# Retention with wide q and k and split output products; another order in two projections; conversions queued behind the MLP's residual

## The chip, the cores and the metric

The kernel runs on one NeuronCore of a Trainium2 chip. The metric is device microseconds for one execution. Times of the kernel before are the median of three runs; the rows further down come from one more execution, which was profiled.

## The reference, cut to what matters

One sequence of 256 tokens with 1024 features passes a block of four token mixers with a squared-ReLU MLP, then a retention layer with a SwiGLU FFN, then a layer of sparse attention (NSA) with a second SwiGLU FFN. All weights are f32 and are used once. What the change touches:

```python
# end of the first block
x = x + jnp.sum(gates * branch, axis=2) @ w_out[l]              # 1024 x 1024
x = x + jnp.square(jax.nn.relu(h @ w_up[l])) @ w_down[l]        # 1024 -> 4096 -> 1024
return rms_norm(x, final_norm_g)
# retention: 4 heads, q and k of 256, v and g of 512, chunk of 128
q = rotate_pairs(q, cos, sin)
k = rotate_pairs(k, cos, sin) * (dk ** -0.5)
scores = jnp.einsum('bhid,bhjd->bhij', qc, kc) * intra_decay
o = jnp.einsum('bhij,bhje->bhie', scores, vc) + ...             # the state's part
# then o is normalised a head, multiplied by silu(g), and projected back (2048 -> 1024)
# NSA: q, three gates a head, keys and values of three branches; projected back (1024 -> 1024)
h = h + rms_norm_2(mixed, mix_norm_post[layer])
```

## The kernel before, in words

**Split products.** Nearly every product with weights is made of two parts: an operand is copied by ScalarE to a rounded f32 form (`hi`), VectorE subtracts it from the source (`lo`), and PE multiplies hi by hi, hi by lo and lo by hi (`mm3`, lines 246 to 251). These matmuls take one pass. A matmul of plain f32 operands, as in retention's scores (1136, 1138) and outputs (1164, 1166), is run as two instructions.

**Weights.** `each_half` (225 to 238) loads half a chunk of weights (512 KB) into one of four `raw` buffers through SyncE's DMA queue, ScalarE makes `whi` (234) and VectorE `wlo` (237, in one or two pieces). `whi` and `wlo` have six buffers each (`wsp`); some stages add a few of their own.

**Forms of a projection.** In `ws_tile` (253) the weights stand and the activations stream: per k-step three matmuls of 256 columns. `wide_steps` (265 to 280) makes the same of hi and lo side by side: one matmul of 512 columns (274) with `whi` and one of 256 (276) with `wlo`; the two halves of the bank are then added up by a ScalarE copy (277) and a VectorE addition (278). `an_groups` and `an_steps` let the activations stand and stream weights, 512 columns wide.

**`project_back`** (357 to 383) projects back to 1024 features: two token halves t, two banks of 512 columns each, so four accumulators. The first weight halves go to all four at once. The last three chunks, six halves, are held: t=0 runs all of them for bank 0, then all of them for bank 1, then its residual and norm (`residual`, `nxt.a`) are issued; t=1 follows with both banks for each held half, and before the last half the transposes of the next stage's input for t=0 (`nxt.b(0)`, line 436) are put. `w_out` and `w_no` have eight halves in all (`nk` = 8), `w_ro` 16, the FFNs 22, the MLP 32.

**Residuals.** `add_residual` (446) makes two VectorE additions (449), one a bank. In the MLP a norm with gain follows (406, 411, 414, 416, 1070), and then the next stage's own norm (`Inputs.a`: sums, POOL's power at 416, `xn` at 193 and 194). `Inputs.b` transposes `xn` and makes hi and lo of it (209, 210). The next stage's first weights are loaded and converted meanwhile by `an_groups` (297 to 327); it has eight halves, and in retention one buffer beyond the six.

**Retention.** After v (`w_rv`), q and k of each head are made by `ws_chunk`, rotated by three VectorE products from PSUM and one POOL addition (1124 to 1131), and the scores of the head before are put behind each q (1146). Then for each head the gate is made in four halves (`gates`), the last head's scores or the transposes of the head before follow, and `outputs` multiplies the scores `at` with `v`: one product for t=0 and two for t=1.

**NSA.** It first issues the load of its gate weights `w_ng` and their split to `wg` (1287 to 1290), then `an_groups` for keys and values and the copies of their results to `cd` and `vn` (1304, 1305). `wg` is used later, with `G` in the order of steps.

**Order.** The program's order sets priorities; a scheduler fixes each engine's order when the kernel is built, by what it holds to be ready. `issue_after(i)` makes the instructions traced within it, on i's engine, follow i there; it is an edge of order and no wait. `behind` uses it already in the first block.

Of the kernel before, what the change touches and what calls it, by code (L numbers as in the profile page):

```python
# [19 lines left out]
T = 256  # L20
D = 1024
KT = 8
# [190 lines left out]
class Kernel:  # L213
# [83 lines left out]
    def an_groups(self, groups, n, inp, order=(0, 1), extra=0):  # L297
# [3 lines left out]
        with ExitStack() as es:  # L301
            pool = self.pool(es, "ax_" + groups[0][0], extra) if extra else None
            hs = []
            for i, (name, g) in enumerate(groups):
                for j in range(4):
                    if j % 2 == 0:
                        own = {s: pool for s in range(2) if len(hs) + s + extra >= 4 * len(groups)}
                        chunk = self.each_half(name, 2 * g + j // 2, 4 * n, own, 2)
                    hs.append((i, 2 * j, next(chunk)))
# [47 lines left out]
    def project_back(self, name, nk, get, last, residual, nxt):  # L357


        accs = [[self.bank() for _ in range(2)] for _ in range(2)]  # L360
        n = nk // 2
        held = []
        with ExitStack() as es:
            wx = self.pool(es, "wx_" + name, 2 * last)
            for c in range(n):
                x, k0 = get(c)
                for s, half in enumerate(self.halves(name, c, pools={i: wx for i in range(2) if c >= n - last})):
# [4 lines left out]
                    else:  # L372
                        held.append(a)
            for t in range(2):
                for banks in ((0,), (1,)) if t == 0 or not nxt else ((0, 1),):
                    for a in held[:-1]:
                        self.as_t(accs[t], *a, t, banks)
                    if t and nxt:
                        nxt.b(0)
                    self.as_t(accs[t], *held[-1], t, banks)  # L380
# [89 lines left out]

    def behind(self, engine):
# [5 lines left out]
    def run(self):  # L477
        nc = self.nc
        with ExitStack() as es:
# [9 lines left out]
            self.ps = self.pool(es, "ps", 8, bass.MemoryType.PSUM)  # L489
            nc.scalar.preload_act_table_set("natural_log_exp_and_others")  # L490
# [540 lines left out]
    def mlp(self, inp):  # L1031
# [3 lines left out]
        with ExitStack() as es:  # L1035
# [29 lines left out]
            def residual(t, acc):  # L1065
                self.add_residual(t, acc)
                r = self.sumsq_rstd([self.x[:, t, n * 512:(n + 1) * 512] for n in range(2)], D)
# [22 lines left out]
    def retention(self, inp):  # L1090
        nc, I = self.nc, self.I
        mm = nc.tensor.matmul
        with ExitStack() as es:
# [30 lines left out]
            def rotated(s, ps):  # L1124
                a = tp.tile([128, 2, T], F32, tag=f"rot{s}", name="rot")
                b = tp.tile([128, 2, T], F32, tag="rotb", name="rotb")
                nc.vector.tensor_tensor(a, ps, cs, op=OP.mult)
                for j in range(2):
                    nc.vector.tensor_tensor(b[:, j, :], ps[:, 1 - j, :], sn[:, j, :], op=OP.mult)
# [12 lines left out]
            for h in range(4):  # L1142
                rot = []
                for s in range(2):
                    rot.append(rotated(s, self.ws_chunk("w_rqk", 2 * h + s, xin)))
                    if s == 0 and qk:
# [4 lines left out]
            def gates(g):  # L1151
                sg = tp.tile([128, 2, 512], F32, tag="sg", name="sg", bufs=1)
                for _ in self.an_steps("w_rg", g, 512, xin,
                                       lambda t, ps: nc.scalar.activation(sg[:, t, :], ps, AF.Silu)):
                    pass
                return sg

            def outputs(g, sg):
                vs = slice(g * 512, (g + 1) * 512)
# [443 lines left out]
```

## Time and profile before

| what | us |
|---|---|
| median of three runs (lowest, highest) | 1204.8 (1204.67, 1211.26) |
| the profiled execution, by the device's time | 1208.24 |
| its span, first to last instruction | 1206.5 |
| mean granted TensorE clock (of full speed) | 0.993 |

The stages lie as follows in the profiled execution: the mixers to 267 us, `w_out` to 291, the MLP to 480, retention to 690 with its q and k from 526 to 576 and the gates and outputs to 640, the first FFN to 876, NSA to 1014 with `w_no` from 987, the second FFN to the end. PE is TensorE's matmul, PEld its weight loads, DVE VectorE, ACT ScalarE, POOL GpSimd. A matmul's shown duration overlaps with the next; the distance between two starts is what one costs. PEclk is the clock that PE was granted, 1.00 for 2.4 GHz.

### The profile page before, as it was taken

How to read it: one execution, taken by the hardware profiler on the slowest of the kernel's cores; microseconds unless marked ns; L12 is line 12 of the kernel's file. 1: busy time of each engine (PE TensorE's matmuls, PEld its weight loads, DVE VectorE, ACT ScalarE, POOL GpSimd, SP SyncE). 2: the span in 40 equal slices, each digit the busy share in tenths (PEclk: the TensorE clock that was granted, in tenths of full speed). 3: DMA queues.
4: the chain of work that ended last, by engine and by line, in shares of the span. 5: the costliest groups of instructions: out<-in, count | busy, mean ns of one | idle time of the engine just before them, and what ended most of it. 6: DMA issues, size and time to landing. Idle time of an engine off the chain costs nothing.

```text
span 1206.5 us, 18129 instructions
## 1 busy us (share of the span) xinstructions
PE 1184.8 (98%) x6848; PEld 1014.4 (84%) x6848; DVE 806.3 (67%) x1413; ACT 662.9 (55%) x1148; POOL 80.8 (7%) x87
## 2 busy tenths in 40 slices
PE   8999999999999998999999999999999999999997
PEld 6999889887888887899878888888889877888886
DVE  7757877667746667557456665657778967655663
ACT  5545765655644454543555554556567876645561
POOL 1000001200000000012000000000100530000000
PEclk8999999999999999999999999999999999999999
DMA  7654454536455565554546355556655226555560
GB/s 239 196 175 158 140 191 158 175 126 230 161 192 187 191 208 181 177 194 158 166 148 213 120 192 189 192 185 212 209 194 179 72 70 205 179 189 186 189 205 35
DMA packets 60775, 210.11 MB, mean 174 GB/s; under 512 B 7120, under 2 KB 9808, under 8 KB 60560
## 3 DMA queue, kind: packets, MB, share of 16 engines
q1 hardware_dynamic: 60688, 208.95, 53.0%
q8 instruction: 54, 0.88, 0.3%
q14 instruction: 33, 0.27, 0.1%
HBM read 207.84 MB, written 1.08 MB: 173 GB/s over the span
## 4 chain that ended last, share of the span: by engine, by line
PE 82%; DVE 7%; DMA 5%; ACT 3%; issue 1%; POOL 0%; SPq 0%; DVEq 0%; POOLq 0%; ACTq 0%
PE b L274 19%; PE b L249 15%; PE b L251 15%; PE b L250 15%; PE b L276 9%; DVE wlo L237 3%; ACT whi L234 1%; PE b L436 1%; DMA raw<-w_up 1%; DMA raw<-w_no 1%; DMA raw<-w_rv 1%; PE b L1536 1%; DMA raw<-w_ck 1%; DMA wng<-w_ng 1%; ACT s L1503 1%
## 5 line engine op out<-in xcount | busy, mean ns | idle before, releaser
L237 DVE TENSOR_TENSOR wlo<-raw,whi 128x1024 fp32r<-128x1024 f32 (+3 forms) x432 | 470.9, 1103 | 265.1 <-ACT whi L234 262.2
L234 ACT ACTIVATE whi<-raw 128x1024 fp32r<-128x1024 f32 (+1 forms) x384 | 401.6, 1050 | 383.6 <-issue 116.5
L274 PE MATMUL b<-x,whi 128*128 128x512 f32 x1024 | 362.7, 398 | 0.0
L276 PE MATMUL b<-x,wlo 128*128 128x256 f32 x1024 | 286.3, 280 | 0.0
L249 PE MATMUL b<-whi,x 128*128 128x512 f32 (+1 forms) x720 | 283.9, 395 | 1.8 <-ACT x L209 1.0
L250 PE MATMUL b<-wlo,x 128*128 128x512 f32 (+1 forms) x720 | 280.7, 390 | 1.0 <-DVE wlo L237 0.8
L251 PE MATMUL b<-whi,x 128*128 128x512 f32 (+1 forms) x720 | 279.8, 390 | 0.6 <-DVE x L210 0.6
L274 PEld LDWEIGHTS b<-x,whi 128*128 128x128 f32 x1024 | 192.2, 188 | 45.9 <-issue 0.3
L276 PEld LDWEIGHTS b<-x,wlo 128*128 128x128 f32 x1024 | 193.1, 189 | 0.9
L249 PEld LDWEIGHTS b<-whi,x 128*128 128x128 f32 x720 | 136.1, 189 | 34.5 <-ACT x L209 4.3
L251 PEld LDWEIGHTS b<-whi,x 128*128 128x128 f32 x720 | 136.3, 189 | 29.9 <-DVE x L210 1.3
L250 PEld LDWEIGHTS b<-wlo,x 128*128 128x128 f32 x720 | 136.4, 189 | 28.7 <-DVE wlo L237 1.9
L249 PE MATMUL b<-x,whi 128*128 128x256 f32 x480 | 137.6, 287 | 0.0
L251 PE MATMUL b<-x,wlo 128*128 128x256 f32 x480 | 135.5, 282 | 0.4 <-DVE wlo L237 0.4
L250 PE MATMUL b<-x,whi 128*128 128x256 f32 x480 | 135.4, 282 | 0.0
L249 PEld LDWEIGHTS b<-x,whi 128*128 128x128 f32 x480 | 91.5, 191 | 2.1 <-issue 1.5
L251 PEld LDWEIGHTS b<-x,wlo 128*128 128x128 f32 x480 | 91.5, 191 | 0.6 <-DVE wlo L237 0.6
L250 PEld LDWEIGHTS b<-x,whi 128*128 128x128 f32 x480 | 91.6, 191 | 0.1
L416 POOL TENSOR_TENSOR rstd<-ms,mhalf 128x1 f32<-128x1 f32 x22 | 13.8, 626 | 686.5 <-DVE ms L414 686.5
L210 DVE SCALAR_TENSOR_TENSOR x<-b,gc,x 128x128 fp32r<-128x128 f32 x112 | 36.7, 348 | 20.2 <-ACT x L209 18.3
L209 ACT ACTIVATE x<-b,gc 128x128 fp32r<-128x128 f32 x112 | 37.9, 367 | 21.7 <-PE b L436 16.5
L1503 ACT ACTIVATE s<-s,nm 128x128 f32<-128x128 f32 (+1 forms) x64 | 28.2, 444 | 2.6 <-DVE rz L1507 1.4
(277 smaller groups left out, 1014.8 us busy)
## 6 DMA issues: line engine op xcount, KB each, us to landing
raw<-w_fi SPq DMA_DIRECT2D x88, 512.0 KB, 4.5
raw<-w_fo SPq DMA_DIRECT2D x44, 512.0 KB, 4.5
raw<-w_gate SPq DMA_DIRECT2D x32, 512.0 KB, 4.2
raw<-w_up SPq DMA_DIRECT2D x32, 512.0 KB, 3.9
raw<-w_down SPq DMA_DIRECT2D x32, 512.0 KB, 3.9
raw<-w_qk SPq DMA_DIRECT2D x24, 512.0 KB, 4.1
raw<-w_rv SPq DMA_DIRECT2D x16, 512.0 KB, 4.8
raw<-w_rqk SPq DMA_DIRECT2D x16, 512.0 KB, 4.5
```

What stands on the lines that cost most here:

```text
L209: k.nc.scalar.activation(hi, ps[:, j, :], AF.Copy, scale=g)
L210: k.nc.vector.scalar_tensor_tensor(lo, ps[:, j, :], g, hi.bitcast(F32), op0=OP.mult, op1=OP.subtract)
L234: nc.scalar.activation(hi[:, :n], r, AF.Copy)
L237: nc.vector.tensor_tensor(lo[:, c], r[:, c], hi[:, c].bitcast(F32), op=OP.subtract)
L249: mm(out, lhs[0], rhs[0], start=start, stop=False)
L250: mm(out, lhs[0], rhs[1], start=False, stop=False)
L251: mm(out, lhs[1], rhs[0], start=False, stop=stop)
L274: mm(ps.rearrange("p a t -> p (a t)"), half[0][:, s], x[2][:, k].rearrange("p a t -> p (a t)"), start=k == 0, stop=False)
L276: mm(ps[:, 0], half[1][:, s], x[0][:, k, :], start=False, stop=k == KT - 1)
L416: nc.gpsimd.tensor_tensor(r, ms, self.mhalf[:, :1], op=OP.pow)
L436: self.nc.tensor.transpose(ps[:, j, :], src[:, j * 128:(j + 1) * 128], self.ident)
L1503: nc.scalar.activation(s[:, a, i, :], s[:, a, i, :], AF.Exp, bias=nm[:, a, i:i + 1], scale=-1.0, accum_out=z[:, a, i:i + 1])
```

## The change

`project_back` runs t=0 (and t=1 of the last projection) in another order where it has eight halves: bank 0 leads bank 1 by one held weight. It resets `rows_done`; only the MLP's residual for t=0 sets it, to the last ScalarE and VectorE instructions issued so far, and `an_groups` queues the conversions of its third half and all later ones behind these two. Retention makes q and k by `ws_wide` and rotates them from SBUF; the scores of a head are put behind the next head's k (for the last head behind the second gate half). Its `gates` splits v and the scores of its head into hi and lo, in the buffers of the rotations, behind the third gate half for the first head and behind the first for the others, and `outputs` makes each product of three one-pass matmuls. NSA's split of `wg` is issued behind the copies of `cd` and `vn` and queued behind them. Loads, tiles and the rest stay as they are.

```diff
@@ an_groups
+                    queued = self.queued(self.rows_done if len(hs) > 1 else ())
                     if j % 2 == 0:
                         own = {s: pool for s in range(2) if len(hs) + s + extra >= 4 * len(groups)}
                         chunk = self.each_half(name, 2 * g + j // 2, 4 * n, own, 2)
-                    hs.append((i, 2 * j, next(chunk)))
+                    with queued:
+                        hs.append((i, 2 * j, next(chunk)))
@@ project_back
+        self.rows_done = ()
...
+            lead = min(len(held), 1 if nk == KT else len(held))
             for t in range(2):
-                for banks in ((0,), (1,)) if t == 0 or not nxt else ((0, 1),):
-                    for a in held[:-1]:
-                        self.as_t(accs[t], *a, t, banks)
-                    if t and nxt:
+                if t == 0 or not nxt:
+                    order = [(i, 0) for i in range(lead)]
+                    for i in range(len(held)):
+                        order += [(i + lead, 0)] * (i + lead < len(held)) + [(i, 1)]
+                else:
+                    order = [(i, n) for i in range(len(held)) for n in range(2)]
+                for i, n in order:
+                    if t and nxt and (i, n) == (len(held) - 1, 0):
                         nxt.b(0)
-                    self.as_t(accs[t], *held[-1], t, banks)
+                    self.as_t(accs[t], *held[i], t, (n,))
@@ new
+    def lasts(self):
+        order = list(reversed(self.nc.cur_bb.bb.instructions))
+        return [next(i for i in order if i.engine == e.engine) for e in (self.nc.scalar, self.nc.vector)]
+    def queued(self, instructions):
+        es = ExitStack()
+        for i in instructions:
+            es.enter_context(self.tc.issue_after(i))
+        return es
@@ mlp, residual
                 self.add_residual(t, acc)
+                if t == 0:
+                    self.rows_done = self.lasts()
@@ retention
-            def rotated(s, ps):
-                a = tp.tile([128, 2, T], F32, tag=f"rot{s}", name="rot")
+            def rotated(s, i):
+                a = self.ws_wide("w_rqk", i, xin, tp.tile([128, 2, T], F32, tag=f"rot{s}", name="rot"))
                 b = tp.tile([128, 2, T], F32, tag="rotb", name="rotb")
-                nc.vector.tensor_tensor(a, ps, cs, op=OP.mult)
                 for j in range(2):
-                    nc.vector.tensor_tensor(b[:, j, :], ps[:, 1 - j, :], sn[:, j, :], op=OP.mult)
+                    nc.vector.tensor_tensor(b[:, j, :], a[:, 1 - j, :], sn[:, j, :], op=OP.mult)
+                nc.vector.tensor_tensor(a, a, cs, op=OP.mult)
                 nc.gpsimd.tensor_tensor(a, a, b, op=OP.add)
...
-                    if s == 0 and qk:
+                    if s == 1 and qk:
                         scores(h - 1, *qk)
...
+                parts, steps = [], 0
                 for _ in self.an_steps("w_rg", g, 512, xin,
                                        lambda t, ps: nc.scalar.activation(sg[:, t, :], ps, AF.Silu)):
-                    pass
-                return sg
+                    steps += 1
+                    if steps == 2 and g == 0:
+                        scores(3, *qk)
+                    if steps == (3 if g == 0 else 1):
+                        src = [v[:, t, g * 512:(g + 1) * 512] for t in range(2)] + [at[:, g, :]]
+                        for tag, x in zip(("rot0", "rot1", "rotb"), src):
+                            hl = [tp.tile([128, 2, T], F32, tag=tag, name=tag).rearrange("p a t -> p (a t)").bitcast(F32R)
+                                  [:, :x.shape[1]] for _ in range(2)]
+                            self.split(*hl, x)
+                            parts.append(hl)
+                return sg, parts
...
-                    mm(p, at[:, g, t * 128:t * 128 + 128], v[:, 0, vs], start=True, stop=t == 0)
+                    self.mm3(p, [x[:, t * 128:t * 128 + 128] for x in w], v0, True, t == 0)
                     if t:
-                        mm(p, at[:, g, T:384], v[:, 1, vs], start=False, stop=True)
+                        self.mm3(p, [x[:, T:384] for x in w], v1, False, True)
@@ nsa
-            wg = tp.tile([128, KT, 96], F32R, name="wg")
-            self.split(wg[:, :, :48], wg[:, :, 48:], raw.rearrange("p (k c) -> p k c", k=KT))
...
                 nc.scalar.activation(vn[:, t, :], ps[1][t], AF.Copy)
+            wg = tp.tile([128, KT, 96], F32R, name="wg")
+            with self.queued(self.lasts()):
+                self.split(wg[:, :, :48], wg[:, :, 48:], raw.rearrange("p (k c) -> p k c", k=KT))
```

## Rows read from the trace of the kernel before

**Rows 1.** The page's first part, PE: busy us (share), count of instructions.

```profile
PE 1184.8 (98%) x6848; PEld 1014.4 (84%) x6848; DVE 806.3 (67%) x1413; ACT 662.9 (55%) x1148; POOL 80.8 (7%) x87
```

**Rows 2.** Waits of PE, whole span: who waited for whom, us, times, longest.

```profile
PE b L436 <- DVE xn L193: 7.9, 2, 4.6
PE b L249 <- ACT whi L234: 1.5, 2, 0.8
PE b L249 <- ACT x L209: 1.0, 3, 0.5
```

**Rows 3.** Timeline of PE, end of the MLP: start, us, engine, line, operation.

```profile
473.54 0.40 PE L251 MATMUL b<-whi,x 128*128 128x512 f32 x1
```

**Rows 4.** Chain of waits, 462 to 481 us: start, us, what.

```profile
468.89 1.07 ACT whi L234
...
469.98 1.29 DVE wlo L237 x2
471.27 0.61 DVE res L449
...
477.28 1.94 PE b L436 x8
479.23 0.43 PE b L249
```

**Rows 5.** Windows: stretch, length, busy us by engine, PEclk, DMA share, GB/s.

```profile
478.00:480.00 2.00, 2.00 (x9) 1.81 (x8) 0.69 (x3) 0.99 (x3) 0.00 (x0) 0.51 0.00 0
...
998.00:1002.00 4.00, 3.44 (x9) 2.66 (x10) 2.52 (x3) 1.80 (x3) 0.00 (x0) 0.60 0.78 265
```

**Rows 6.** Timeline of PE in `w_no`; in brackets the wait before.

```profile
987.36 0.50 PE L249 MATMUL b<-whi,x 128*128 128x512 f32 x1
...
995.80 0.47 PE L249 MATMUL b<-whi,x 128*128 128x512 f32 x1
997.04 0.50 PE L250 MATMUL b<-wlo,x 128*128 128x512 f32 x1 [0.76 <-DVE wlo L237]
...
998.56 1.03 PE L249 MATMUL b<-whi,x 128*128 128x512 f32 x2 [0.79 <-ACT whi L234]
...
1011.86 1.04 PE L436 MATMUL b<-cm,xn 128*128 128x128 f32 x8
```

**Rows 7.** Timeline of PE in `w_out`.

```profile
266.90 0.40 PE L249 MATMUL b<-whi,mx 128*128 128x512 f32 x1
...
288.92 1.03 PE L436 MATMUL b<-cm,xn 128*128 128x128 f32 x8
```

**Rows 8.** Timeline of VectorE in `w_out`.

```profile
282.44 1.89 DVE L237 TENSOR_TENSOR wlo<-raw,whi 128x512 fp32r<-128x512 f32 x3
284.24 0.68 DVE L449 TENSOR_TENSOR res<-res,b 128x512 f32<-128x512 f32 x1
```

**Rows 9.** Timeline of ScalarE at the start of the NSA layer.

```profile
877.60 0.52 ACT L242 ACTIVATE wg<-wng 128x384 fp32r<-128x384 f32 x1 [0.78 <-DMA wng<-w_ng]
```

**Rows 10.** Timeline of PE, retention's q and k: two chunks between these.

```profile
557.03 0.36 PE L249 MATMUL b<-x,whi 128*128 128x256 f32 x1
...
568.63 1.02 PE L1136 MATMUL b<-rot 128*128 128x256 f32 x4
```

**Rows 11.** Timeline of PE, first FFN: ten wide k-steps between these.

```profile
706.62 0.40 PE L274 MATMUL b<-x,whi 128*128 128x512 f32 x1
...
710.15 0.40 PE L274 MATMUL b<-x,whi 128*128 128x512 f32 x1
```

**Rows 12.** Timeline of PE, outputs of retention's first head.

```profile
587.91 1.88 PE L1164 MATMUL b<-v,at 128*128 128x512 f32 x4
589.63 1.02 PE L1166 MATMUL b<-v,at 128*128 128x512 f32 x2
```

**Rows 13.** Window of the gate stage: PE, PEld, DVE, ACT, POOL busy, PEclk.

```profile
576.00:640.00 64.00, 64.00 (x281) 49.36 (x280) 33.86 (x40) 33.13 (x50) 4.94 (x5) 1.00 0.47 149
```

**Rows 14.** Instructions on tile `wg`: ns min/median/max, first and last start.

```profile
L1366 PE MATMUL b<-x,wg x8: 278/280/282, 907.0 to 908.8; 128*96 128x256 f32 x8
```

More of the change, by code (lines that the diff above doesn't have):

```diff
@@ L489, in run @@
             self.ps = self.pool(es, "ps", 8, bass.MemoryType.PSUM)
+            self.rows_done = ()
             nc.scalar.preload_act_table_set("natural_log_exp_and_others")
@@ L1144, in retention @@
                 for s in range(2):
-                    rot.append(rotated(s, self.ws_chunk("w_rqk", 2 * h + s, xin)))
-                    if s == 0 and qk:
+                    rot.append(rotated(s, 2 * h + s))
+                    if s == 1 and qk:
                         scores(h - 1, *qk)
@@ L1152, in gates, with outputs @@
                 sg = tp.tile([128, 2, 512], F32, tag="sg", name="sg", bufs=1)
+                parts, steps = [], 0
                 for _ in self.an_steps("w_rg", g, 512, xin,
                                        lambda t, ps: nc.scalar.activation(sg[:, t, :], ps, AF.Silu)):
-                    pass
-                return sg
-            def outputs(g, sg):
-                vs = slice(g * 512, (g + 1) * 512)
+                    steps += 1
[9 more added lines that the diff above has]
+                return sg, parts
+            def outputs(g, sg, parts):
+                v0, v1, w = parts
                 ss = self.st.tile([128, 2], F32, tag="ss2", name="ss2")
@@ L1186, in retention @@
                 sg = gates(g)
-                if g == 0:
-                    scores(3, *qk)
-                else:
+                if g:
                     transposed(yn)
-                yn = outputs(g, sg)
+                yn = outputs(g, *sg)
             e1.close()
```

## The prediction

> **What bounds the kernel now.** I read the page's engine table first: TensorE (PE) is busy 98% of the span [rows 1], so time can only be won where PE runs a product more cheaply or where it stands still. Next the waits of PE alone [rows 2]: they name the three kinds of place that the change touches. PE waits for `xn` before transposes (4.6 us of the 7.9 is the start of the kernel, the other 3.3 lies at the end of the MLP), for the high parts of weights (twice, once in each of the two projections with eight weight halves), and for `x` (three times, 0.5 at most).
>
> The largest is at the end of the MLP. PE's last matmul of t=1 before the transposes starts at 473.54 [rows 3] and, at 0.23 us, ends at 473.77. The transposes start at 477.28 and the next matmul at 479.23 [rows 4]. Eight transposes take 1.03 us where nothing holds them [rows 6], so that matmul could have started at 474.8: it is 4.4 us late, and it takes 0.43 instead of 0.23, as the next one does, 0.4 more. Together 4.8 us. The reader is to see two things here. In the chain of waits [rows 4] the transposes wait for vector work that begins with the residual addition at 471.27, and that addition sits behind a weight conversion (469.98) whose own source landed only when the copy at 468.89 could start. And the clock: from 478 to 480 us PE was granted 0.51, that is the 1.2 GHz level, after it had stood still; from 998 to 1002, also behind waits, it was 0.60 [rows 5], a mix of the two levels.
>
> In `w_no`, 90 matmuls (24 direct, 36 of t=0, 30 of t=1) lie between 987.36 and the transposes at 1011.86 [rows 6]. The first 37 of them take 8.44 us, 0.228 each; 90 would take 20.5, and 24.5 passed: 4.0 us lost, in the waits before 997.04 and 998.56 and at the lower clock behind them. In `w_out` the same 90 take from 266.90 to 288.92, 22.0 us [rows 7]: 1.5 lost.
>
> **The change part by part.** All terms are PE time, made against the profiled execution (1208.24, span 1206.5); it lies 3.4 us above the median 1204.8, and I subtract the sum from the median.
>
> *MLP's conversions behind the residual.* Seven halves of `w_rv` fit in the weight buffers; numbers 2 to 6 now stand behind both additions of t=0 on VectorE (on ScalarE they stand behind a weight copy that comes earlier anyway). Bank 1 of t=0 is complete when t=1's 30 matmuls begin, at 473.77 − 30 × 0.228 = 466.9. From the second addition to the transposes the chain took 477.28 − 471.27 = 6.0 us, so it would end at 473.0, and PE arrives at 473.77: the whole 4.8 could go. What is late next: ten pieces of conversion (five halves at 1.29 for two pieces [rows 4], 6.4 us) that VectorE did while it had nothing else now fall among the chains of t=0 and t=1, and every piece in front of a step delays it by up to 0.65. How a filled chain looks is seen in `w_out`, where three pieces stand in front of the second addition (282.44 to 284.24) [rows 8]. I take 0.7 for what the first chain then runs past PE's arrival and 0.6 for the second, whose cover is six halves, 36 × 0.228 = 8.2 us. SP's next loads wait for these raw buffers too, but the first half that this delays is the seventh that PE uses. Gain 3.5; bounds: 4.8, and −2.1 if all ten pieces stood in the first chain (473.0 + 6.4 = 479.4, against 477.28).
>
> *One weight's lead in the projections with eight halves.* Products of bank 1 now stand between those of bank 0, so PE has work when a weight is late. In `w_no` the sixth held weight's high part is there just before 998.56 [rows 6] and its low part one conversion (1.29 [rows 4]) later, 999.8. With the lead PE has 24 + 27 matmuls before it, 987.36 + 51 × 0.228 = 999.0, so it waits 0.6 at most instead of twice, and the clock may hold. 4.0 − 0.6 leaves 3.4. Against it: bank 0 of t=0 now ends one product before bank 1 instead of six, so the normalisation starts with both at once and then queues among `w_fi` conversions that may still wait for their DMAs. I take 0.8 for that: gain 2.6, bounds 0 and 4.0. In `w_out` the wait goes likewise, but the second addition came at 284.24 [rows 8] though bank 1 was complete at 288.92 − 30 × 0.228 = 282.1: the conversions in front of it set the transposes, and nothing queues these. Gain 0.9, bounds 0 and 1.5. Projections with more halves lead by all of them, which is the order as it was, and so does t=1 where a next stage follows: nothing.
>
> *Retention's q and k, wide.* Per k-step three matmuls of 256 columns become one of 512 and one of 256. Two chunks, 32 k-steps, take 557.03 to 568.63: 0.3625 each [rows 10]. The FFN's wide form takes 706.62 to 710.15 for ten: 0.353 [rows 11]. 128 k-steps × 0.0095 = 1.2 us gained. Bounds: 0, since both forms stream 768 columns, and 2.6, if those ran at the rate of `w_no` (1.5 × 0.228 = 0.342). The Trainium skill, "TensorE: Matmul & The Clock Gate", section "Back-to-back issue gap", makes a matmul cost its columns at 2.4 GHz plus about 2.5 ns: by that rule a k-step would save one 2.5 ns and the edit an estimated 0.3 us instead of 1.2. The trace does not agree with it (0.121 and 0.228 a matmul, above the rule's 0.109 and 0.216), so the rows decide. The copy and the addition of each half, and rotations that now read SBUF, are ScalarE and VectorE time, dealt with below. The scores come one chunk later, with as much PE work behind them as before: nothing.
>
> *Outputs as three matmuls.* Each f32 product of 512 columns is run as two passes, 0.43 apart: four in 1.72 us from 587.91 [rows 12]. Twelve products make 24 × 0.43 = 10.3 us; as 36 single passes at 0.228 they take 8.2. Gain 2.1; at the wide form's rate (0.353 × 2/3 = 0.235 a pass) 1.8. Added: three splits a head, each a ScalarE copy (0.52 for 384 columns [rows 9]) and a VectorE subtraction (0.65, as a piece in rows 4). Cover: of the 64 us of the gate stage VectorE is busy 33.9 and ScalarE 33.1 [rows 13]; 12 × 0.65 = 7.8 fits into either, and so do 16 additions and 16 copies of half that size in the q and k stage. From the second head on they are issued behind the first of four gate halves, 6 us or more ahead of their use; for the first head behind the third, with one half in hand. If this cover were gone it would cost what the slower rival below says.
>
> *Gate split later.* ScalarE stands 0.78 us at 877.60 for the gate weights' DMA while copies of `x` queue behind it [rows 9], and PE then waits 0.5 for such a copy [rows 2]. The split now stands behind the copies of `vn` and `cd`; its product starts at 907.0 [rows 14], long after. The DMA keeps its place. Gain 0.5; bounds 0.8, and −0.5 if the split then delays a later conversion that PE meets.
>
> Sum: 3.5 + 2.6 + 0.9 + 1.2 + 2.1 + 0.5 = 10.8; 1204.8 − 10.8 = **1194.0 us**.
>
> **The rivals.** (1) *The waits only move.* The chains of t=0 end no earlier, because additions or normalisations still queue behind conversions that wait for DMAs, as in `w_out`. Then the MLP gives 1.3, `w_no` 0.8, `w_out` 0: with 1.2, 2.1 and 0.5 a sum of 5.9, 1198.9 us. For it: rows 8, and that the order on each engine is fixed before the DMA times are known. Against: the edge in the MLP takes away just that. Where that edge binds nothing, this is the outcome too.
> (2) *All waits go, and the clock stays at 2.4 GHz.* 4.8 + 4.0 + 1.5 + 2.6 + 2.1 + 0.8 = 15.8, 1189.0 us. For it: PE was at the lower clock only behind such waits [rows 5]. Against: the 6.4 us of pieces must go somewhere.
> (3) *Slower: the splits land late.* Place: the end of each gate group in retention. If ScalarE takes a head's splits only after its last conversions, PE waits for three copies and one subtraction, some 4 × 0.65 = 2.6 us, before each head's outputs, and then runs 4 us at 0.60 [rows 5], 1.6 more: 4 × 4.2 = 16.8 us against 10.8 gained, 1210.8 us. It decides from the point where the last low part lands after the fourth gate half's last matmul. Against it: the idle time in rows 13.
>
> **How the numbers follow.** My forecast has 0.43, rival 1 0.31, rival 2 0.20, rival 3 0.06. The range 1188.5 to 1203.5 holds the first three nearly whole; its upper end is rival 1 with `w_no`'s gain gone, the gate split at its bad end and some 3 us lost to the MLP's pieces. About 1% is what a measurement of this kernel can tell from no change: faster means below 1192.8. That is rival 2 and 0.3 of the forecast's share, 0.33; slower, above 1216.8, is rival 3 with a wait in a second place, 0.04; between them 0.63.
>
> **What would show it.** Right: no wait of PE for `xn` over 1 us near 470, the clock at 1.00 there and near 1000; the MLP's residual additions directly after each bank, with low-part pieces behind them; the 90 matmuls of `w_no` in about 21.5 us; retention's k-steps at 0.353 and one head's outputs in 2.1 us, with their splits done before. Wrong: the wait for `xn` stands at t=1's transposes instead; PE waits for a split operand; matmuls slow from 0.23 to 0.43 in a place that was clean before.

## The result and the profile after

| kernel | us, median (lowest to highest) | runs | ratio to before (95% interval) |
|---|---|---|---|
| before, beside it | 1204.8 (1204.53 to 1211.26) | 5 | |
| changed | 1197.88 (1197.15 to 1199.3) | 5 | 0.9931 (0.9915 to 0.9948) |

That is 8.3 us less by the ratio (0.0069 × 1204.8) and 6.9 by the medians, against 10.8 forecast. The kernel before spreads over 7 us here and the changed one over 2, and a median of five of the former says little: in later measurements it was 1207.25 (28 runs), 1206.44 (17) and 1206.8 (10). I go by the ratio; the changed kernel once more (`after2`, below), beside 17 runs of the kernel before, gives 8.2 by the medians.

The page's engine table of the changed kernel (profiled execution 1197.15 us, span 1195.4, clock 0.996), and the waits of PE over the span:

```profile
PE 1177.3 (98%) x6732; PEld 1007.0 (84%) x6732; DVE 819.9 (69%) x1441; ACT 672.7 (56%) x1176; POOL 81.4 (7%) x87
```
```profile
PE b L445 <- DVE xn L193: 7.5, 3, 5.2
...
PE b L249 <- ACT x L209: 0.8, 3, 0.3
PE b L250 <- DVE wlo L237: 0.5, 1, 0.5
```

PE lost 7.5 us of busy time against [rows 1] and VectorE gained 13.6 (the splits, the wide form's additions). The waits for high parts of weights of [rows 2] are gone. The waits for `xn` are not: without the 5.2 of the start, 2.3 us are left, now at two places instead of one.

**The end of the MLP.** VectorE from the second residual addition of t=0 to `xn` (L458 is the addition, L1094 the gain, L237 the pieces of low parts), then PE's transposes of t=0 and of t=1:

```profile
465.09 0.69 DVE L458 TENSOR_TENSOR res<-res,b 128x512 f32<-128x512 f32 x1 [3.43 <-PE b L251]
465.70 0.68 DVE L237 TENSOR_TENSOR wlo<-raw,whi 128x512 fp32r<-128x512 f32 x1
466.30 0.68 DVE L420 CUSTOM_DVE_ANT_0 junk<-res 128x512 bf16<-128x512 f32 x1
...
468.76 1.41 DVE L1094 SCALAR_TENSOR_TENSOR res<-res,rstd,gain 128x512 f32<-128x512 f32 x2 [0.44 <-POOL rstd L425]
470.09 0.69 DVE L237 TENSOR_TENSOR wlo<-raw,whi 128x512 fp32r<-128x512 f32 x1
...
472.04 0.68 DVE L237 TENSOR_TENSOR wlo<-raw,whi 128x512 fp32r<-128x512 f32 x1
473.16 0.49 DVE L193 TENSOR_SCALAR xn<-res,rstd 128x512 f32<-128x512 f32 x1 [0.44 <-POOL rstd L425]
```
```profile
473.79 1.06 PE L445 MATMUL b<-cm,xn 128*128 128x128 f32 x8 [0.95 <-DVE xn L193]
...
483.70 1.09 PE L445 MATMUL b<-cm,xn 128*128 128x128 f32 x8
```

The addition waited for nothing but PE. From it to the transposes 8.7 us passed (473.79 − 465.09) instead of the 6.0 of [rows 4], since six pieces now stand between the steps. PE waited 0.95, and t=1's transposes not at all. The clock held:

```profile
476.00:478.00 2.00, 2.00 (x10) 1.56 (x9) 2.00 (x8) 1.58 (x7) 0.00 (x0) 1.00 0.79 220
478.00:480.00 2.00, 2.00 (x10) 1.64 (x9) 2.00 (x7) 0.83 (x3) 0.86 (x1) 1.00 0.99 343
```

Where [rows 5] had 0.51, PEclk is 1.00; VectorE is busy for the whole of both windows.

**`w_no`.** ScalarE around the sum of squares of the next stage's norm (L415), then PE:

```profile
993.60 1.06 ACT L234 ACTIVATE whi<-raw 128x1024 fp32r<-128x1024 f32 x1
996.47 1.06 ACT L234 ACTIVATE whi<-raw 128x1024 fp32r<-128x1024 f32 x1 [1.81 <-DMA raw<-w_fi]
997.44 0.61 ACT L415 ACTIVATE junk<-res 128x512 bf16<-128x512 f32 x1
```
```profile
989.74 0.50 PE L250 MATMUL b<-wlo,x 128*128 128x512 f32 x1 [0.50 <-DVE wlo L237]
...
999.96 1.09 PE L445 MATMUL b<-cm,xn 128*128 128x128 f32 x8 [1.32 <-DVE xn L193]
```

Of the two waits of [rows 6] one of 0.50 is left, but a new one of 1.32 stands at the transposes. The sum sits behind a copy of the FFN's weights that itself waited 1.81 for its DMA, which looks like the cause. VectorE, which makes the additions (L470), the other half's sum and `ms` from both sums (L423), shows that it hardly counts:

```profile
994.98 1.42 DVE L470 SCALAR_TENSOR_TENSOR res<-xn,rstd,res 128x512 f32<-128x512 f32 x2
...
997.52 0.69 DVE L237 TENSOR_TENSOR wlo<-raw,whi 128x512 fp32r<-128x512 f32 x1
998.18 0.21 DVE L423 TENSOR_SCALAR ms<-ss 128x1 f32<-128x1 f32 x1
...
999.42 0.49 DVE L193 TENSOR_SCALAR xn<-res,rstd 128x512 f32<-128x512 f32 x1 [0.43 <-POOL rstd L425]
```

`ms` follows VectorE's own piece without a wait; three such pieces stand between the additions and `xn`.

**Retention.** The last 32 k-steps of q and k start behind the scores at 556.84, as [rows 10] does at 557.03, and the outputs of the first head at 581.79:

```profile
556.84 0.48 PE L274 MATMUL b<-x,whi 128*128 128x512 f32 x1
...
568.24 0.59 PE L1160 MATMUL b<-rot 128*128 128x256 f32 x2
...
581.79 0.39 PE L249 MATMUL b<-rot,rotb 128*128 128x512 f32 x1
...
583.84 0.39 PE L249 MATMUL b<-whi,x 128*128 128x512 f32 x1
```

32 k-steps take 11.40 us instead of 11.60, so 0.2 a head and 0.8 in all. Nine passes take 2.05, 0.228 each, where six passes of [rows 12] took 6 × 0.43 = 2.58. No wait for a split operand is among PE's waits. The other heads' outputs stand behind transposes and take 2.17, 0.41 less: 0.53 + 3 × 0.41 = 1.8.

**Stages.** One profile misleads here, so all fourteen of this study stand in one table. Each number is the distance between two starts of PE, in us: `w_out` from its first product and `w_no` from the last product before it to t=1's transposes, the MLP from there to the next t=1's transposes, retention from there to the last transposes of `yn`, NSA from t=1's transposes to the first product with `wg`. The labels are those of the experiments.

| profile | parts of the change | w_out | MLP | retention | NSA to `wg` | w_no |
|---|---|---|---|---|---|---|
| before | none | 35.55 | 186.58 | 150.09 | 32.06 | 37.15 |
| again | none | 34.48 | 188.61 | 150.07 | 31.80 | 35.47 |
| o_queue | MLP's queue | 33.88 | 183.26 | 150.15 | 32.03 | 35.63 |
| o_lead | lead | 34.00 | 186.87 | 150.05 | 31.49 | 34.97 |
| o_ret | retention | 34.09 | 186.06 | 147.33 | 32.93 | 35.15 |
| o_wg | gate split | 34.26 | 187.74 | 150.07 | 30.70 | 35.27 |
| after | all | 33.44 | 183.26 | 147.35 | 30.70 | 35.77 |
| after2 | all | 33.87 | 183.26 | 147.39 | 30.70 | 35.38 |
| u_lead | all but the lead | 33.92 | 183.26 | 147.38 | 30.71 | 36.75 |
| u_ret | all but retention | 34.13 | 183.27 | 150.11 | 30.70 | 35.59 |
| a_xn | all, queue moved | 35.14 | 185.95 | 147.34 | 30.66 | 35.13 |
| a_no | all, queue in `w_no` too | 34.46 | 183.25 | 147.37 | 30.72 | 35.83 |
| a_pool | all, two pieces on POOL | 34.21 | 183.21 | 147.30 | 30.67 | 34.81 |
| a_j | all, ScalarE's order in `w_no` | 34.04 | 183.26 | 147.34 | 30.67 | 34.56 |

Read down a column: retention has two values, with and without its edit, and they agree within 0.1. The MLP and NSA have one value with the edit and a spread without it. In `w_out` and `w_no` the spread (2.1 and 2.6) is larger than any difference between the orders.

`w_out` hides two changes that nearly cancel. From its first product to t=0's transposes it takes 20.7 to 21.6 us in the eight profiles with the lead and 21.7 to 22.2 in the six without, 0.9 less by the means. From there to t=1's it takes 13.1 instead of 12.4 by the means: PE waits for a part of `x` there in all eight, and in three of the six.

### The profile page after: what moved, and what is told of

The parts are those of the page before. It is cut to its first block, busy times and chain, and to the rows that moved or that the text cites. A ratio compares the mean times of both kernels' runs of the same rounds, so it can differ in the third digit from the quotient of the medians.

```text
span 1195.4 us, 17977 instructions
## 1 busy us (share of the span) xinstructions
PE 1177.3 (98%) x6732; PEld 1007.0 (84%) x6732; DVE 819.9 (69%) x1441; ACT 672.7 (56%) x1176; POOL 81.4 (7%) x87
## 4 chain that ended last, share of the span: by engine, by line
PE 86%; DVE 7%; ACT 3%; DMA 2%; issue 1%; POOL 0%; SPq 0%; DVEq 0%; POOLq 0%; ACTq 0%
PE b L274 22%; PE b L249 15%; PE b L251 15%; PE b L250 15%; PE b L276 11%; DVE wlo L237 3%; PE b L445 1%; DMA raw<-w_fi 1%; ACT whi L234 1%; PE b L1570 1%; DMA raw<-w_v 1%; ACT s L1537 1%; PE b L1553 1%; DMA raw<-w_up 0%; PE b L668 0%
## 5 line engine op out<-in xcount | busy, mean ns | idle before, releaser
L237 DVE TENSOR_TENSOR wlo<-raw,whi 128x1024 fp32r<-128x1024 f32 (+3 forms) x432 | 470.1, 1100 | 245.4 <-ACT whi L234 242.4
L274 PE MATMUL b<-x,whi 128*128 128x512 f32 x1152 | 408.2, 398 | 0.0
L274 PEld LDWEIGHTS b<-x,whi 128*128 128x128 f32 x1152 | 216.3, 188 | 51.8 <-issue 0.3
L249 PE MATMUL b<-x,whi 128*128 128x256 f32 x352 | 101.2, 287 | 0.0
L250 PE MATMUL b<-x,whi 128*128 128x256 f32 x352 | 99.2, 282 | 0.0
L249 PEld LDWEIGHTS b<-x,whi 128*128 128x128 f32 x352 | 67.0, 190 | 2.1 <-issue 1.5
L250 PEld LDWEIGHTS b<-x,whi 128*128 128x128 f32 x352 | 67.0, 190 | 0.1
```

The lines of the kernel that those rows point to most:

```text
L237: nc.vector.tensor_tensor(lo[:, c], r[:, c], hi[:, c].bitcast(F32), op=OP.subtract)
L249: mm(out, lhs[0], rhs[0], start=start, stop=False)
L250: mm(out, lhs[0], rhs[1], start=False, stop=False)
L274: mm(ps.rearrange("p a t -> p (a t)"), half[0][:, s], x[2][:, k].rearrange("p a t -> p (a t)"), start=k == 0, stop=False)
```

## The experiments

**The kernel before once more, and three parts alone.** The edits are the hunks of the change as they stand in the diff: `o_queue` those of `an_groups`, the resets and marks of `rows_done` and the two new functions; `o_lead` the order in `project_back`; `o_ret` the retention layer.

> The kernel before, unchanged, profiled a second time. In the two profiles the changed kernel's span is 11.1 us shorter (1206.5 to 1195.4), by the medians 6.9. Theory: the first profiled execution of the kernel before was 3.4 us longer than its median at one place that varies from execution to execution (a wait behind a DMA, with the lower clock after it); this profile then shows 1203 to 1204 us of span and one or two of the touched places shorter: the MLP's end (wait for xn 3.3), w_no (90 matmuls in 24.5), w_out (22.0) or the start of NSA (32.1 from its second transposes to the gate product). Rival: the places are the same within 0.3 us in every execution, and the 3.4 us lie outside them, in the first 267 us or in the second FFN (175.5).

Measured 0.9996 (0.9984 to 1.0009), 1207.32 us. Its profile shows how bad the MLP's end can be without the queue: the transposes waited 3.85 us, and the clock came back later than in [rows 5]:

```profile
476.00:478.00 2.00, 1.59 (x8) 1.62 (x9) 0.33 (x2) 0.87 (x2) 0.00 (x0) 0.50 0.00 0
478.00:480.00 2.00, 2.00 (x7) 1.62 (x6) 1.23 (x4) 1.25 (x4) 0.00 (x0) 0.50 0.00 0
480.00:482.00 2.00, 2.00 (x7) 1.52 (x6) 1.93 (x6) 1.24 (x4) 0.00 (x0) 0.50 0.29 41
```

It also shows `w_no` without the wait for a weight of [rows 6] and without its loss of the clock: 35.47 us against 37.15. Of the 4.0 us that I wanted to win there, 1.8 were not lost in this execution (22.9 us to the transposes against 24.7), and PE lost part of the rest at the transposes, where it waited 1.48. The places differ by up to 2 us between two executions, so the rival is out; the theory's span of 1203 to 1204 us did not come either (1205.5).

> The kernel before with the queue behind the MLP's residual alone. Theory (the edge frees the residual chain, the pieces then fill it): the wait of PE for xn near 477 falls from 3.3 to about 1 and the clock stays at 1.00; from the MLP's second transposes to retention's second transposes 3.3 us less than 186.6; 1201.5 us by the median. Rival (the two additions were late for the DMA alone and the chain only moves): wait 3 or more, 1204.8.

Measured 0.9964 (0.995 to 0.9979), 4.3 us less; by the stage, 183.26 against a mean of 187.17 in the five profiles without the queue, 3.9. PE's wait there was 0.95: the theory.

> The kernel before with the lead of one weight alone, in w_out and w_no. Theory: the waits for weights go, w_out's 90 matmuls take 21.0 instead of 22.0 and the next 12.4 instead of 13.5 to the following transposes; w_no's take 23.2 instead of 24.7 counted from the last attention product, with 1.3 us of wait moved to the transposes; 3.5 us in all, 1201.3 by the median. Rival (the order on VectorE and ScalarE is drawn anew and that made the 12.4, not the lead): w_out 21.0, the following stretch still 13.5, 1202.4.

Measured 0.9986 (0.9973 to 0.9999), 1.7 us with an interval from 0.1 to 3.3; by the medians 0.6. `w_out` took 20.9 us to t=0's transposes, as expected, and the next ones came 13.1 behind them, nearer the rival's 13.5 than the theory's 12.4. In `w_no` the wait moved to the transposes, as in the changed kernel, and here VectorE did wait for ScalarE's sum:

```profile
1008.71 1.09 PE L442 MATMUL b<-cm,xn 128*128 128x128 f32 x8 [1.25 <-DVE xn L193]
```
```profile
1006.92 0.21 DVE L420 TENSOR_SCALAR ms<-ss 128x1 f32<-128x1 f32 x1 [0.54 <-ACT junk L412]
```

> The kernel before with retention's part alone (wide q and k, split outputs, its scores moved). Theory: 128 k-steps at 0.3546 instead of 0.3618 save 0.9, the outputs at 2.14 a head instead of 2.58 save 1.8; 2.7 us from retention's second transposes to the last transposes of yn (150.1 before), nothing elsewhere; 1202.1 by the median. Rival (other places are ordered anew by it): the stage gives 2.7 and another stretch between transposes moves by 1 us or more.

Measured 0.9956 (0.9941 to 0.9972), 5.3 us (3.7 by the medians), more than the stage shows (2.75). The two were set against each other by `u_ret`.

**The changed kernel once more, and the gate split alone.** `o_wg` is the kernel before with the hunk of NSA and the helper functions.

> The changed kernel once more, with five rounds, as the yardstick for the two runs beside it and to see how far one execution's waits can be trusted. Expected: 0.993 of the kernel before, with 0.991 to 0.995 as before. In the profile: w_out about 21.0 us from the first product to the transposes, the MLP's end without a drop of the clock, retention from t=1's transposes to the last transposes of yn 147.3 us. For w_no the six profiles read so far differ by up to 2.3 us with the same order (24.70, 22.93, 23.08, 22.64 in the old order, 22.41 and 23.16 in the new): theory A (the lead of one weight is worth 2.6 us in w_no) expects about 22 us here; theory B (the wait only moves to the transposes, behind conversions that wait for a DMA) expects 22.4 to 23.2 and a wait of PE for xn of 1 us or more there.

Measured 0.993 (0.9917 to 0.9943), 1198.25 us. `w_no` took 22.8 us to the transposes (35.38 with t=1), where PE waited 1.78, and ScalarE shows the same order as in the changed kernel's first profile: theory B.

> The kernel before with the split of NSA's gate weights alone moved behind the copies of vn and cd. Theory A (the prediction's term: the split's wait for its DMA holds up one copy of x): 0.5 us, 0.9996 of the kernel before. Theory B (as the changed kernel's profile reads: two waits go, 0.5 for x and 0.6 for xs, since the split's 1.3 us of VectorE work also stood before xs): the stretch from t=1's transposes to wg takes 30.7 us instead of 31.8 to 32.1, 1.1 to 1.4 us less, 0.999 of the kernel before. Rival C: the change of that stretch came from another part of the change, and it stays at 31.5 to 32.9.

Measured 0.999 (0.9981 to 0.9998), 1.2 us, and 30.70 in its stage: theory B. The mean of the five profiles without the edit is 32.06, so 1.4. The forecast had counted one of the two waits. This is the other, in the kernel before:

```profile
903.18 0.38 PE L1366 MATMUL b<-whi,xs 128*120 128x256 f32 x1 [0.62 <-DVE xs L243]
```

Neither is in a profile with the edit.

**VectorE's pieces taken out of the MLP's chain.**

```diff
                 if nxt:
                     nxt.a(t)
+                    if t == 0 and self.rows_done:
+                        self.rows_done = [self.rows_done[0], self.lasts()[1]]
```

> The changed kernel, but on VectorE the MLP's conversions stand behind xn of t=0 instead of behind the second residual addition; ScalarE's place is unchanged. Theory A (the 0.95 us that PE still waits at the MLP's transposes come from the pieces of low parts that stand in each step of the chain from the addition to xn): the chain takes 6.0 to 6.5 us instead of 8.7, the wait goes to 0, and PE starts the transposes 0.9 us earlier; total 0.5 to 1.0 us less than the changed kernel (0.9992 to 0.9996 of it). Theory B (VectorE has no slack behind the chain: what is not converted in it comes later): the chain is as short, but PE then waits for a low part of w_rv or for xn of t=1 by 1 us or more, and the total is the same or up to 2 us longer.

Measured 0.9953 (0.994 to 0.9966), 1200.81 us, 2.6 more than the changed kernel beside it. Its six runs lie in two heaps, three near 1199 and three near 1202.5; the profiled one is of the upper. VectorE's chain and what follows it, then PE:

```profile
466.92 0.69 DVE L460 TENSOR_TENSOR res<-res,b 128x512 f32<-128x512 f32 x1 [3.44 <-PE b L251]
...
472.46 0.49 DVE L193 TENSOR_SCALAR xn<-res,rstd 128x512 f32<-128x512 f32 x1 [0.66 <-POOL rstd L427]
472.86 3.69 DVE L237 TENSOR_TENSOR wlo<-raw,whi 128x512 fp32r<-128x512 f32 x6
```
```profile
473.59 1.04 PE L447 MATMUL b<-cm,xn 128*128 128x128 f32 x8
...
481.83 0.50 PE L249 MATMUL b<-whi,x 128*128 128x512 f32 x1 [1.15 <-ACT x L209]
...
488.21 1.09 PE L447 MATMUL b<-cm,xn 128*128 128x128 f32 x8 [1.06 <-DVE xn L193]
```

Both theories were half right. The chain took 6.7 us instead of 8.7 and PE did not wait at the transposes, so the pieces are what made up the remaining 0.95. But the six pieces then stood in one block, 3.69 us, before `x` and t=1's chain, and the stretch from t=0's transposes to t=1's grew from 9.9 to 14.6. Of these 4.7, 0.9 are four products that PE does in front of t=0's transposes in the changed kernel and behind them here.

**Conversions queued in `w_no` as well.**

```diff
                 if nxt:
                     nxt.a(t)
+                    if t == 0 and name == "w_no":
+                        self.rows_done = self.lasts()
```

> The changed kernel, with the conversions of the second FFN's weights (from the third half on) queued behind w_no's xn of t=0 on both engines, as the MLP's are. Theory A (in w_no the gain of the lead is given back at the transposes, because the sum of squares on ScalarE stands behind a copy that waits for the DMA of w_fi): the wait of 1.3 us for xn goes, the 90 matmuls of w_no take about 21.7 us instead of 23.2, and the total falls by 1.0 to 1.5 us. Theory B (the conversions are as long, and only later): the transposes come earlier by as much, but PE waits for a high or low part of w_fi in the first products of the FFN by 1 us or more, and the total stays within 0.5 us or grows.

Measured 0.9944 (0.9932 to 0.9956), 1.8 us more than the changed kernel beside it: theory B, though low parts alone cost less than its 1 us. The transposes of t=0 came after 20.9 us, without a wait, t=1's 14.9 behind them instead of 12.6. PE waited 0.74 for `x`, and the FFN's first products met low parts that were late, three times like this (0.8 in all):

```profile
1011.63 0.50 PE L250 MATMUL b<-wlo,x 128*128 128x512 f32 x1 [0.30 <-DVE wlo L237]
```

Without pieces between the additions and `xn` the chain was short, 3.8 us from the first addition to the transposes (999.55 − 995.73) instead of 5.0 (999.96 − 994.98):

```profile
995.73 1.41 DVE L472 SCALAR_TENSOR_TENSOR res<-xn,rstd,res 128x512 f32<-128x512 f32 x2
```
```profile
999.55 1.03 PE L447 MATMUL b<-cm,xn 128*128 128x128 f32 x8
```

**One edit undone in the changed kernel.** `u_lead` has the old order of `project_back`, `u_ret` the old retention; the rest is the changed kernel.

> The changed kernel with the old order of products in w_out and w_no (bank 0 complete before bank 1). Theory A (by the stages of ten profiles the lead is worth little: w_out 22.0 against 21.0 us to the transposes, of which 0.7 is given back behind them, and w_no 22.9 against 22.8): the total is 0 to 1.0 us longer than the changed kernel, 0.9935 of the kernel before, w_out and w_no at 21.7 to 22.2 and 22.6 to 23.2 us. Theory B (the prediction's terms, 3.5 us for both, or the 1.7 that the lead alone gave): 1.5 to 3.5 us longer, 0.9945 to 0.996, and w_no at 24 us or more with PE waiting for high parts of weights.

Measured 0.9927 (0.9911 to 0.9944), 1198.69 us, not to be told from the changed kernel: theory A for the total. In `w_out` PE waited 0.89 for a high part, which the lead removes, yet the stretch is 33.92, in the middle of those with the lead. In `w_no` it took 36.75, but no wait for a weight stood there. PE waited at the transposes. Here the norm in front of the additions was late: its sum over bank 1 (L411) stood behind two copies of weights, and VectorE then did four pieces before the next step. From the first addition (997.86) to the transposes it took 4.93, as in the changed kernel:

```profile
993.16 2.04 ACT L234 ACTIVATE whi<-raw 128x1024 fp32r<-128x1024 f32 x2
995.11 0.58 ACT L411 ACTIVATE junk<-b 128x512 bf16<-128x512 f32 x1
```
```profile
1002.79 1.09 PE L439 MATMUL b<-cm,xn 128*128 128x128 f32 x8 [2.44 <-DVE xn L193]
```

> The changed kernel with retention as it was: narrow q and k, outputs of f32. Theory A (retention gives what its stage shows, 0.9 by q and k and 1.8 by the outputs): the stretch from t=1's transposes to the last transposes of yn takes 150.1 us instead of 147.35, and the total is 2.7 us longer, 0.9953 of the kernel before. Theory B (the edit alone measured 5.3 us, so it also gives something outside its stage, at the end of the MLP or in the first FFN): 4 us or more longer, 0.9965 or above, with the MLP's end or w_ro slower than in the changed kernel.

Measured 0.9958 (0.9943 to 0.9974), 1201.75 us; 0.0028 above the changed kernel's 0.993, 3.4 us, with intervals that overlap. The stage is 2.75 us longer (150.11 against 147.36) and no other differs by more than its spread: theory A, as far as the stages go. Why the edit alone measured 5.3 us stays open. In its one profile two other places were short, the time up to `w_out`'s first product (265.7 us; 266.0 to 267.3 in the others) and the MLP (186.06; 186.58 to 188.61 in the others without the queue); that the edit does this is not shown.

**Less work for VectorE at the MLP's end.** In `each_half`:

```diff
-                nc.vector.tensor_tensor(lo[:, c], r[:, c], hi[:, c].bitcast(F32), op=OP.subtract)
+                e = nc.gpsimd if (name, i, s) == ("w_rv", 1, 1) else nc.vector
+                e.tensor_tensor(lo[:, c], r[:, c], hi[:, c].bitcast(F32), op=OP.subtract)
```

> The changed kernel, but the two pieces of the low part of w_rv's fourth half are made by POOL instead of VectorE. Theory A (at the MLP's end VectorE has no idle time between 465 and 482 us, so the order of its work only moves waits, and only less work on it helps): the chain from the second addition to the transposes takes 7.5 us instead of 8.7, the wait of 0.95 falls below 0.2, t=1's transposes come no later, and the MLP's stretch falls from 173.35 to 172.4 to 172.8; total 0.5 to 1.0 us less, near the limit of what five rounds show. Theory B (POOL is slow beside a busy VectorE: its additions of the same size took 1.3 to 2.3 us in retention, so a piece takes 2 us or more and stands before POOL's power of the norm): PE waits for xn or for this low part, and the stretch is the same or longer.

Measured 0.9921 (0.9903 to 0.9938), not to be told from the changed kernel, and 183.21 in the stage: neither theory. POOL had done both pieces before the residual, in 2.55 us, well ahead of its power; and VectorE still has a piece behind the addition:

```profile
459.21 2.55 POOL L238 TENSOR_TENSOR wlo<-raw,whi 128x512 fp32r<-128x512 f32 x2 [163.16 <-ACT whi L234]
467.55 0.93 POOL L426 TENSOR_TENSOR rstd<-ms,mhalf 128x1 f32<-128x1 f32 x1 [5.79 <-DVE ms L424]
```
```profile
464.84 0.69 DVE L459 TENSOR_TENSOR res<-res,b 128x512 f32<-128x512 f32 x1 [3.43 <-PE b L252]
465.45 0.68 DVE L238 TENSOR_TENSOR wlo<-raw,whi 128x512 fp32r<-128x512 f32 x1
...
472.91 0.48 DVE L193 TENSOR_SCALAR xn<-res,rstd 128x512 f32<-128x512 f32 x1 [0.45 <-POOL rstd L426]
```

The place that the two pieces left was filled by the next ones: from the addition to `xn` it is 8.07 us, as in the changed kernel (473.16 − 465.09). The chain is as long as the order makes it, one piece in each gap, so long as there are pieces.

**ScalarE's order alone in `w_no`.** `rows_from` is 1 elsewhere:

```diff
                 if nxt:
                     nxt.a(t)
+                    if t == 0 and name == "w_no":
+                        order = [i for i in reversed(self.nc.cur_bb.bb.instructions) if i.engine == self.nc.scalar.engine]
+                        self.rows_done, self.rows_from = order[1:2], 3
...
-                    queued = self.queued(self.rows_done if len(hs) > 1 else ())
+                    queued = self.queued(self.rows_done if len(hs) > self.rows_from else ())
```

> The changed kernel, with ScalarE's copies of w_fi from the fourth half on queued behind the sum of squares of the next stage's norm for t=0 in w_no, and nothing queued on VectorE. Theory A (the wait of 1.3 us for xn at w_no's transposes comes from one copy that waits for its DMA in front of that sum): the sum moves up by about 1 us, the transposes come 0.5 to 1.0 us earlier (w_no 21.9 to 22.4 us instead of 22.8 to 23.2), what follows them stays at 12.6 us, and the total falls by as much. Theory B (VectorE's pieces hold the chain as much as ScalarE's copy does, or the later copies are missed behind it, as when all conversions were queued): w_no stays above 22.5 us, or the stretch behind it grows past 13 us.

Measured 0.9918 (0.99 to 0.9936), 1197.18 us, the lowest of the study. ScalarE, then PE, then VectorE:

```profile
993.58 1.06 ACT L234 ACTIVATE whi<-raw 128x1024 fp32r<-128x1024 f32 x1 [0.33 <-DMA raw<-w_fi]
995.36 0.63 ACT L418 ACTIVATE junk<-res 128x512 bf16<-128x512 f32 x1 [0.72 <-DVE res L473]
...
997.42 1.06 ACT L234 ACTIVATE whi<-raw 128x1024 fp32r<-128x1024 f32 x1 [0.26 <-DMA raw<-w_fi]
```
```profile
999.45 1.09 PE L448 MATMUL b<-cm,xn 128*128 128x128 f32 x8 [0.94 <-DVE xn L193]
```
```profile
994.52 1.41 DVE L473 SCALAR_TENSOR_TENSOR res<-xn,rstd,res 128x512 f32<-128x512 f32 x2
...
997.67 0.20 DVE L426 TENSOR_SCALAR ms<-ss 128x1 f32<-128x1 f32 x1
...
998.91 0.49 DVE L193 TENSOR_SCALAR xn<-res,rstd 128x512 f32<-128x512 f32 x1 [0.44 <-POOL rstd L428]
```

The sum now waits for its source and not for a weight, 2.7 us earlier if both are counted from the start of the stretch (17.9 us behind it against 20.6). `w_no` took 22.0 us to the transposes and what follows stayed at 12.6: theory A by its numbers, 1.0 us less than the changed kernel's two profiles (35.58 − 34.56). Its reason does not hold. From the first addition to the transposes it took 4.93 us (999.45 − 994.52), against 4.98 in the changed kernel and 4.97 in `after2`: VectorE's three pieces hold the chain as much as the sum did, which is theory B's reason. What came earlier is the additions, 17.1 us behind the start of the stretch instead of 18.2 and 17.9. `a_pool` and `o_lead` have them as early (17.1 and 16.9) without this edit, and `a_pool`'s stage is only 0.25 longer. In `o_lead`, where VectorE waited for the sum, the chain took 5.56, so the edit can take up to some 0.6 us out of an execution. The total fits (0.9918 against 0.993), but their intervals overlap: that the edit makes `w_no` or the kernel faster is not shown.

## Why the prediction was right, and where it was off

The direction and the size held: 1197.88 lies in the range (1188.5 to 1203.5) and within 1% of the kernel before, the case with 0.63. The gain of 8.3 lies half way between the forecast (10.8) and its first rival (5.9), and by place it is a mixture of the two.

| term | forecast | by the stages |
|---|---|---|
| MLP's queue | 3.5 | 3.9 |
| lead in `w_no` | 2.6 | 0.6, unsure |
| lead in `w_out` | 0.9 | 0.2, unsure |
| q and k wide | 1.2 | 0.8 |
| outputs of one-pass matmuls | 2.1 | 1.8 |
| gate split | 0.5 | 1.4 |
| sum | 10.8 | 8.7 |

- **MLP: right, by its own steps.** The addition came directly behind its bank, pieces fell among the chain, and what it then ran past PE's arrival was 0.95 (0.7 forecast); the clock held. That the 0.95 is so near is partly luck: PE now does four more of t=1's products in front of the transposes (34 of 36, where the kernel before does 30), 0.9 us of cover that the forecast did not count. Without them the wait would be an estimated 1.9. The 0.6 for the second chain did not come. `a_xn` shows that the pieces are the price: out of one chain, they stand in the next.
- **`w_no`: the mis-sized term.** The step that failed is "4.0 − 0.6 leaves 3.4". The 4.0 came from one execution, and `again` lost neither that much nor the clock. The means of the profiles are 35.9 in the old order (six) and 35.3 in the new (six, without `a_no` and `a_j`), less than the spread of either. The 90 matmuls took 22.2 to 23.2 us in these six, and not about 21.5. The 0.8 for the normalisation behind `w_fi` named the right place and was too small: with the weights in time, t=0's banks are complete earlier, and then PE waited 1.2 to 2.0 at the transposes in each of the six. What holds the chain from the additions on is chiefly VectorE's own pieces (4.9 us with three of them in `a_j` and 3.8 without in `a_no`, the sum in front in both); ScalarE's sum behind a late weight adds 0 to some 0.6 (4.97 in `after2`, 5.56 in `o_lead`).
- **`w_out`: the first rival's number, not its reason.** It gave 0, and the stretch does not get shorter that one can tell; `u_lead` without the edit measured the same total. But the rival had t=0's chain end no earlier, and t=0's transposes do come 0.9 earlier, just as forecast. The step that the forecast left out is what follows: 0.7 is lost again up to t=1's transposes, where PE waits for parts of `x`.
- **Retention: right, both a little smaller.** The 0.353 of the FFN's rows is reached inside a chunk, but a chunk's edges take the rest, so 32 k-steps save 0.20 and not 0.30. By the rule of the Trainium skill that the prediction weighed ("TensorE: Matmul & The Clock Gate", "Back-to-back issue gap") it would have been an estimated 0.3 in all; 0.8 was measured, so the rows (1.2) came a little nearer. That section gives the rule for a single matmul, and for a stream of weight loads and matmuls, which this is, a shorter time (0.131 us at 512 columns); the 0.228 measured here agrees with neither. The outputs run at 0.228 a pass as forecast; heads two to four pay 0.1 behind transposes. Their splits were early each time, so the slower rival had nothing to hold it.
- **Gate split: too small.** The forecast priced ScalarE's stall and the wait for `x`, and left out the wait for `xs`, which was in the same view of PE's waits; `o_wg` shows both going together.

The misses of the other five terms (+0.4, −0.7, −0.4, −0.3, +0.9) nearly cancel, so the 2.0 of `w_no` is the difference of the two sums. Of the 3.9 us between 1194.0 and 1197.88, 2.5 is gain that did not come (10.8 − 8.3), and 1.4 is the median from which I subtracted: 1204.8 × 0.9931 is 1196.5, and 1204.8 lay below every later median of the kernel before.

## What to carry to other kernels

A wait that hangs on a DMA differs from one execution to the next: before pricing its removal, look at it in two or three profiles of the same kernel, by stage, and price the mean. Where a chain of small steps shares an engine with conversions, ask what fills its gaps: an edge behind the chain's first step takes away the long wait, an edge behind its last step only moves it to the next chain. And measure the chain itself before naming what holds it: in `w_no` a sum behind a late weight looked like the cause, yet the chain took 4.93 us without that and 4.97 and 4.98 with it, because VectorE's pieces held it as long. Queueing everything cost more than it won there.

## What the runs showed beyond this

- With the queue the MLP's stretch is the same within 0.1 us in eight profiles that leave its place alone (183.21 to 183.27), and without it 186.06 to 188.61. So the edge made this stage steadier as well as shorter. For the whole kernel that is not shown: the ten runs of `o_queue` spread over 6.2 us, the eleven of `o_wg`, without the queue, over 2.7.
- PE's waits of 0.95 and 1.32 in the changed kernel cost no clock (1.00 in the windows behind them), nor did the 2.44 in `u_lead`. The 2.47 at the MLP's end in `o_ret` did: 0.50 from 474 to 476 us. After the wait of 3.85 in `again` PEclk stood at 0.50, the 1.2 GHz level, for three windows of 2 us.
- POOL's subtraction of 128x512 took 1.28 us (two in 2.55) where VectorE's took 0.68. The one VectorE instruction beside them, an addition, took its usual 0.69.
- The second FFN's stretch from t=1's transposes to the end took 175.5 to 175.7 in four profiles and 176.1 or more in ten, with either kernel; its cause was not looked for. Both profiles of the kernel before are among the four and both of the changed kernel among the ten, so that some 0.6 us of the difference between their spans is lost there.
